# Issuing scores and value products one at a time between a unit's matmuls, in a one-core encoder block

## The chip, the cores and the metric

The kernel runs on one core of one Trainium2 chip. The time is the device time of one execution, in microseconds (us); the time of a kernel is the median of its runs. The engines are named as in the profile: PE is TensorE (matmuls; PEld its weight loads), DVE is VectorE, ACT is ScalarE, POOL is GpSimd, SP is SyncE, which here only issues transfers. Each engine works through its own instructions in the order in which the program wrote them and waits by semaphore for the others.

## The reference, cut to what matters

One encoder block on x of 256 tokens by 2048 channels, all in float32:

```python
h = rmsnorm(x, norm1_g)
q, k, v, u = split(h @ w_in)               # 12 q heads, 4 k and v heads of 128; u: 4 groups of 128
a = window_attention(q, k, v, sink)        # |t - s| <= 128, ALiBi, a sink logit per head
f = real(fft2(u, over positions and group channels)) @ w_fourier    # per group
x = x + concat(rmsnorm(a), rmsnorm(f)) @ w_out
h = rmsnorm(x, norm2_g)
gate, val = split(h @ w_up)                # 5504 each
x = x + (gelu(conv3(gate) + b) * val) @ w_down
y = rmsnorm(x, normf_g)
```

Attention is softmax over 256 keys for each of 12 heads: scores are q·k, masked and biased, the exponentials are divided by their sum plus that of the sink, and the result is multiplied by v.

## The kernel before

**Units.** The weights stream from memory in tiles of 128x2048 float32. Each tile is one *unit* of the first part: units 0 to 3 the u projection, 4 to 7 the v projection, 8 to 23 the k and q projections in the order k0 q0 q1 q2 k1 q3 … q11 (`QK_ORDER`), 24 to 39 the output projection. The feed-forward part follows and is not touched. A float32 product is made of three faster ones: every operand is split into a high part `hi` (a ScalarE copy to the faster format, L197) and the remainder `lo` (a VectorE subtraction, L205), and hi·hi, hi·lo and lo·hi are added. In a q/k unit (`still_weights`, L361) the weights stand in the array and the tokens stream: 16 matmuls of hi weights over 512 columns (both parts of the tokens) and 16 of lo weights over 256, alternately. In an output unit (`moving_weights`, L349) the tokens stand and 512 columns of weights stream, 24 matmuls.

**What sets the order.** The order on each engine is written out by hand in three tables of steps, `before`, `beside` and `behind`. `unit(i)` (L399) runs the steps of `before[i]`, issues the unit's matmuls, runs `beside[i]`, then `step(i)`, which issues the split of unit i+2 and the load of a later tile on SP, and then `behind[i]`. No scheduler moves anything: a step's place in these tables is its place in the order of every engine that it uses.

**The heads' steps.** A head whose q projection is unit s passes through these steps. At s+1, qk_out adds the two halves of its product and qk_parts splits it into qT (ScalarE, then VectorE). At s+2, `scores` (L743) makes six matmuls of 128x256 in `before`, `scores_out` masks them and takes the row maximum on VectorE, and `exps` makes exponentials on ScalarE, behind the split. At s+3, `weigh` divides them (VectorE L790) and `flip_out` transposes blocks of 32 (VectorE L336) and sends them to memory; at s+4 `flip_in` fetches them back turned. `flip_parts` splits the result into `pt` one unit ahead of `values`. `values` (L836) makes six matmuls of 128x256 with v in `before`, 7 units after the projection for heads 0 to 8, 6 for heads 9 and 10, 5 for head 11 (`values_at`), and `values_out` (feature_out: ScalarE square L550 and copy L298, VectorE L299, POOL add L554) puts the scaled parts into `cat`, the tokens of the output projection. Head 11 is not sent through memory: its exponentials are turned by TensorE (`turn`, L797) in `before` of unit 27, right after `weigh` of head 11 in unit 26.

**The Fourier group.** `fourier_rows` (position products, all in unit 9) are copied out by rows_out, two groups in unit 9 and two in unit 10. Then for g = 0 to 3 in unit 10+g: `fourier_channels` (channel products, on TensorE in `before`), `fourier_channels_copy` (ScalarE, beside), `fourier_channels_join` (VectorE L670 to L674, behind), and in unit 11+g `fourier_channels_out` (feature_out). `total_scale` (VectorE L561 to L579 and a POOL power L575) behind unit 25 makes the norm of the Fourier half.

**Buffers.** PSUM has two pools of four banks, `mm` for projections and `dn` for all the small products. The SBUF tags `tmp`, `add` and `sc` have 2, 2 and 4 buffers; the square of feature_out has one.

**Start.** A memset on POOL (L283) writes a 128x128 tile of ones, which TensorE multiplies 7 times (`WARM`) while the first loads are under way.

## Time and profile before

| | |
|---|---|
| median of 3 runs | 933.49 us (933.27 to 934.07) |
| the profiled execution | 933.83 us |
| its span, first to last instruction | 932.1 us |
| mean granted TensorE clock | 0.998 |
| busy PE / PEld / DVE / ACT / POOL | 923.2 / 799.9 / 776.2 / 543.6 / 62.8 us |
| PE's share of the chain that ended last | 98% |

How to read the rows: a row of the timeline has the start and the duration in us, engine, line, operation, output and inputs with their shapes and the count of equal instructions that it groups; at the end, in brackets, the idle time of the engine before it and what ended that. Matmuls overlap in the array, so a matmul's duration is longer than its share of the stream; what counts is the distance from start to start. Equal neighbours are one row (x6), whose duration is from the first start to the last end. Lines are those of the kernel before.

### The profile page before, as it was taken

The numbers are of one execution on the slowest core, as the hardware profiler recorded it, in microseconds if no ns is written. First come the engines' busy times: TensorE is split into PE (matmuls) and PEld (weight loads), VectorE is DVE, ScalarE is ACT, GpSimd is POOL, SyncE is SP. The second block draws the span as 40 slices with busy tenths as digits, with TensorE's granted clock in tenths as the row PEclk, the third lists the DMA queues.
The fourth block names the chain that finished last, engine by engine and source line by source line (L and its number), as shares of the span: only waits on it lengthen the run. The fifth ranks groups of instructions, "written<-read, shape, count | busy, mean of one in ns | idle before, by whom it ended". The sixth has DMA issues, their size and how long they took to land.

```text
span 932.1 us, 12883 instructions
## 1 busy us (share of the span) xinstructions
PE 923.2 (99%) x4973; PEld 799.9 (86%) x4973; DVE 776.2 (83%) x997; ACT 543.6 (58%) x689; POOL 62.8 (7%) x79
## 2 busy tenths in 40 slices
PE   9999999999999999999999999999999999999996
PEld 7888998888888888888888888888888888888885
DVE  7768998787768877898877997888978789989995
ACT  6756777546465655565555665555755556655553
POOL 0101111200000000000000000000000000000002
PEclk9999999999999999999999999999999999999999
DMA  9865777667777668788797769887787968779652
GB/s 361 331 225 158 249 241 215 201 198 269 230 274 256 203 207 256 242 274 263 229 299 251 240 209 298 223 260 233 268 240 244 306 221 269 237 238 272 203 180 91
DMA packets 59597, 225.16 MB, mean 242 GB/s; under 512 B 24465, under 2 KB 30225, under 8 KB 35984
## 3 DMA queue, kind: packets, MB, share of 16 engines
q1 hardware_dynamic: 54928, 194.72, 57.9%
q0 software_dynamic: 4464, 29.36, 17.0%
q8 instruction: 39, 0.64, 0.3%
q10 hardware_dynamic: 144, 0.26, 0.1%
q14 instruction: 22, 0.18, 0.0%
HBM read 216.98 MB, written 7.08 MB: 240 GB/s over the span
## 4 chain that ended last, share of the span: by engine, by line
PE 98%; DMA 0%; ACT 0%; DVE 0%; issue 0%; POOLq 0%; POOL 0%; ACTq 0%
PE ps_gate L372 25%; PE ps_val L372 25%; PE ps_q L372 7%; PE ps_P L1233 4%; PE ps_P L1234 4%; PE ps_P L1232 3%; PE ps_N L1233 3%; PE ps_N L1234 3%; PE ps_N L1232 3%; PE ps_k L372 2%; PE ps_a L357 2%; PE ps_a L355 2%; PE ps_a L356 2%; PE ps_s L748 1%; PE ps_o L842 1%; PE ps_ff L355 1%
## 5 line engine op out<-in xcount | busy, mean ns | idle before, releaser
L205 DVE TENSOR_TENSOR lo<-raw,hi 128x2048 fp32r<-128x2048 f32 (+2 forms) x133 | 295.0, 2221 | 28.3 <-ACT hi L197 28.0
L197 ACT ACTIVATE hi<-raw 128x2048 fp32r<-128x2048 f32 (+1 forms) x131 | 246.8, 1887 | 27.6 <-PE ps_a L356 10.8
L372 PE MATMUL ps_gate<-hU,hi 128*128 128x512 f32 x688 | 236.1, 389 | 0.0
L372 PE MATMUL ps_val<-hU,hi 128*128 128x512 f32 x688 | 236.1, 389 | 0.0
L372 PE MATMUL ps_gate<-hU,lo 128*128 128x256 f32 x688 | 189.9, 276 | 0.0
L372 PE MATMUL ps_val<-hU,lo 128*128 128x256 f32 x687 | 189.6, 276 | 0.0
L372 PEld LDWEIGHTS ps_gate<-hU,hi 128*128 128x128 f32 x688 | 129.2, 188 | 26.8
L372 PEld LDWEIGHTS ps_val<-hU,hi 128*128 128x128 f32 x688 | 129.2, 188 | 26.8
L372 PEld LDWEIGHTS ps_gate<-hU,lo 128*128 128x128 f32 x688 | 129.2, 188 | 1.3
L372 PEld LDWEIGHTS ps_val<-hU,lo 128*128 128x128 f32 x687 | 129.0, 188 | 1.3
L1013 ACT ACTIVATE ft_g<-ps_gate 128x256 f32<-128x256 f32 x43 | 16.5, 384 | 121.1 <-PE ps_gate L372 121.1
L1013 ACT ACTIVATE ft_v<-ps_val 128x256 f32<-128x256 f32 x43 | 16.5, 383 | 87.0 <-PE ps_val L372 87.0
L372 PE MATMUL ps_q<-hT,hi 128*128 128x512 f32 x192 | 65.0, 391 | 0.0
L1232 PE MATMUL ps_P<-hi_P,op_P 128*128 128x512 f32 x144 | 56.0, 389 | 0.0
L1233 PE MATMUL ps_P<-hi_P,op_P 128*128 128x512 f32 x144 | 56.0, 389 | 0.0
L1234 PE MATMUL ps_P<-lo_P,op_P 128*128 128x512 f32 x144 | 56.0, 389 | 0.0
L372 PE MATMUL ps_q<-hT,lo 128*128 128x256 f32 x192 | 51.2, 277 | 0.0
L1130 DVE TENSOR_TENSOR lo_N<-sumw,hi_N 128x2048 fp32r<-128x2048 f32 (+1 forms) x20 | 41.5, 2076 | 9.4 <-ACT hi_N L1129 9.2
L1232 PE MATMUL ps_N<-hi_N,op_N 128*128 128x512 f32 x108 | 42.0, 389 | 0.0
L1233 PE MATMUL ps_N<-hi_N,op_N 128*128 128x512 f32 x108 | 42.0, 389 | 0.0
L1234 PE MATMUL ps_N<-lo_N,op_N 128*128 128x512 f32 x108 | 42.0, 389 | 0.0
L372 PEld LDWEIGHTS ps_q<-hT,hi 128*128 128x128 f32 x192 | 35.2, 188 | 6.6
(415 smaller groups left out, 1592.4 us busy)
## 6 DMA issues: line engine op xcount, KB each, us to landing
raw<-in_w_up SPq DMA_DIRECT2D x86, 1024.0 KB, 6.6
raw<-in_w_in SPq DMA_DIRECT2D x20, 1024.0 KB, 5.4
raw<-in_w_out SPq DMA_DIRECT2D x16, 1024.0 KB, 5.1
sumw<-in_w_down POOLq DMA_DIRECT2D x16, 1024.0 KB, 8.6
raw<-in_w_down_late SPq DMA_DIRECT2D x4, 1024.0 KB, 6.8
raw<-in_w_down_last SPq DMA_DIRECT2D x4, 768.0 KB, 4.0
turnp<-flip SPq DMA_DIRECT2D x44, 64.0 KB, 1.9
flop<-turnp SPq DMA_DIRECT2D x11, 256.0 KB, 3.9
```

The costliest lines, as they stand in the source:

```text
L197: nc.scalar.activation(halves[i][0][:, s], raws[i][:, s], AF.Copy)
L205: nc.vector.tensor_tensor(lo[:, s], raws[i][:, s], f32(hi[:, s]), ALU.subtract)
L355: nc.tensor.matmul(ps, ah, wh, start=first and q == q0, stop=False)
L356: nc.tensor.matmul(ps, al, wh, start=False, stop=False)
L357: nc.tensor.matmul(ps, ah, wl, start=False, stop=last and q == q0 + len(kk) - 1)
L372: nc.tensor.matmul(ps[:, x], (hi, lo)[i][:, k * P : (k + 1) * P], hk(k)[:, x], start=n == 0 and k == 0, stop=n == len(order) - 1 and k == ...
L748: nc.tensor.matmul(ps[:, b * S : (b + 1) * S], qT[:, qo + b * P : qo + (b + 1) * P], kT[:, ko : ko + S], start=n == 0, stop=n == 2,)
L1013: nc.scalar.activation(tmp, ps[:, S : 2 * S], AF.Copy)
L1130: nc.vector.tensor_tensor(lo, src, f32(hi), ALU.subtract)
L1232: nc.tensor.matmul(ps, o[:, 0, p, :], hi[:, s], start=first and p == 0, stop=False)
L1233: nc.tensor.matmul(ps, o[:, 1, p, :], hi[:, s], start=False, stop=False)
L1234: nc.tensor.matmul(ps, o[:, 0, p, :], lo[:, s], start=False, stop=last and p == n - 1)
```

## The change

Scores and products with v are no longer issued as blocks ahead of a unit's matmuls. `scores` and `values` now return lists of six calls each; `unit` puts them on the list `woven`, scores first, and the unit's own loop takes one off it at a time: in a q/k unit after each lo matmul (16 places), in an output unit after each matmul (24 places). `turn` of head 11 stays in `before` of unit 27, now alone there. `values_out` moves behind the split in units below 24 and stays beside, ahead of `weigh`, from unit 24 on. The four channel products all stand ahead of unit 10; their copies and joins come two groups per unit in units 10 and 11, the outs two per unit in 11 and 12; all four rows_out are in unit 9. The warm-up multiplies a constant that the framework provides, 7 times in full and once with half the columns, and the memset of ones is gone. The calls and their shapes are otherwise the same.

```diff
-    ones = base.tile([P, P], F32, tag="ones", name="ones")
-    nc.gpsimd.memset(ones, 1.0)
...
-    ps = bank(dn, "ps_warm")
-    for _ in range(WARM):
-        nc.tensor.matmul(ps[:, 0:P], ones, ones, start=True, stop=True)
+    ps, one = bank(dn, "ps_warm"), nc.const_aps.tensor(1.0, (P, P), F32)
+    for n in [P] * WARM + [P // 2]:
+        nc.tensor.matmul(ps[:, 0:n], one, one[:, 0:n], start=True, stop=True)
...
+    woven = []
+
+    def weave():
+        if woven:
+            woven.pop(0)()
+
     def moving_weights(hi, lo, n, kk, act, b, ps, first, last, q0=0):
...
             nc.tensor.matmul(ps, ah, wh, start=first and q == q0, stop=False)
+            weave()
             nc.tensor.matmul(ps, al, wh, start=False, stop=False)
+            weave()
             nc.tensor.matmul(
                 ps, ah, wl, start=False, stop=last and q == q0 + len(kk) - 1
             )
+            weave()
...
+            if i:
+                weave()
...
     def unit(i, work):
         run(before, i)
+        for f, a in within.pop(i, []):
+            woven.extend(f(*a))
         work(*halves.pop(i))
+        assert not woven
         run(beside, i)
         step(i)
         run(behind, i)
...
         at(before, 9, fourier_rows, g)
-        at(beside, 9 + g // 2, fourier_rows_out, g)
+        at(beside, 9, fourier_rows_out, g)
...
-            i = 10 + g
-            at(before, i, fourier_channels, g)
-            at(beside, i, fourier_channels_copy, g)
-            at(behind, i, fourier_channels_join, g)
-            at(beside, i + 1, fourier_channels_out, g)
-        at(behind, N_OUT + 1, total_scale, sq_f, "f", FW)
+    i = N_QK + 2
+    for g in range(NG):
+        at(before, i, fourier_channels, g)
+        at(beside, i + 1 + g // 2, fourier_channels_out, g)
+    at(behind, N_OUT + 1, total_scale, sq_f, "f", FW)
...
+            at(beside, N_QK + 2 + g // 2, fourier_channels_copy, g)
+            at(behind, N_QK + 2 + g // 2, fourier_channels_join, g)
...
-        for n, h in sorted(heads.items()):
-            if n == values_at(h):
-                at(before, i, values, h)
         if 4 in heads and heads[4] not in FLIPS:
             at(before, i, turn, heads[4])
         if 2 in heads:
-            at(before, i, scores, heads[2])
+            at(within, i, scores, heads[2])
+        now = [h for n, h in sorted(heads.items()) if n == values_at(h)]
+        for h in now:
+            at(within, i, values, h)
...
-        for n, h in sorted(heads.items()):
-            if n == values_at(h):
+        if i >= N_OUT:
+            for h in now:
                 at(beside, i, values_out, h)
...
             at(behind, i, exps, heads[2])
+        if i < N_OUT:
+            for h in now:
+                at(behind, i, values_out, h)
```

More of the change, by code (lines that the diff above doesn't have):

```diff
@@ L1 @@
 from contextlib import ExitStack
+from functools import partial
 import concourse.bass as bass
@@ L386, in step @@
             split(i + ahead)
-    before, beside, behind = {}, {}, {}
+    before, beside, behind, within = {}, {}, {}, {}
     def at(when, i, f, *a):
@@ L694, in block_kernel @@
         at(before, 9, fourier_rows, g)
-        at(beside, 9 + g // 2, fourier_rows_out, g)
+        at(beside, 9, fourier_rows_out, g)
     at(behind, 8, distances)
-    def fourier_channels_steps():
-        for g in range(NG):
-            i = 10 + g
-            at(before, i, fourier_channels, g)
-            at(beside, i, fourier_channels_copy, g)
-            at(behind, i, fourier_channels_join, g)
-            at(beside, i + 1, fourier_channels_out, g)
-        at(behind, N_OUT + 1, total_scale, sq_f, "f", FW)
+    i = N_QK + 2
[3 more added lines that the diff above has]
+    at(behind, N_OUT + 1, total_scale, sq_f, "f", FW)
     ps_v = [bank(mm, f"ps_v{b}") for b in range(2)]
@@ L745, in scores, with one @@
         qT, kT = qk_sb.pop(("q", h)), qk_sb["k", h // GQA]
-        for b in range(2):
-            for n, (qo, ko) in enumerate([(0, 0), (0, S), (S, 0)]):
-                nc.tensor.matmul(
-                    ps[:, b * S : (b + 1) * S],
-                    qT[:, qo + b * P : qo + (b + 1) * P],
-                    kT[:, ko : ko + S],
-                    start=n == 0,
-                    stop=n == 2,
-                )
+        def one(b, n, qo, ko):
+            nc.tensor.matmul(
+                ps[:, b * S : (b + 1) * S],
+                qT[:, qo + b * P : qo + (b + 1) * P],
+                kT[:, ko : ko + S],
+                start=n == 0,
+                stop=n == 2,
+            )
+        parts = [(0, 0), (0, S), (S, 0)]
+        return [partial(one, b, n, *o) for b in range(2) for n, o in enumerate(parts)]
     def scores_out(h):
@@ L839, in values, with one @@
         ps = st["o", h] = bank(dn, f"ps_o{h}")
-        for sb in range(2):
-            for n, (v, q) in enumerate([(v_hi, 0), (v_hi, 1), (v_lo, 0)]):
-                nc.tensor.matmul(
-                    ps[:, 0:S],
-                    v[:, sb, g * HD : (g + 1) * HD],
-                    pt[q][:, sb * S : (sb + 1) * S],
-                    start=sb == 0 and n == 0,
-                    stop=sb == 1 and n == 2,
-                )
+        def one(sb, n, v, q):
+            nc.tensor.matmul(
+                ps[:, 0:S],
+                v[:, sb, g * HD : (g + 1) * HD],
+                pt[q][:, sb * S : (sb + 1) * S],
+                start=sb == 0 and n == 0,
+                stop=sb == 1 and n == 2,
+            )
+        parts = [(v_hi, 0), (v_hi, 1), (v_lo, 0)]
+        return [partial(one, sb, n, *o) for sb in range(2) for n, o in enumerate(parts)]
     def values_out(h):
@@ L855, in values_at, with fourier_channels_steps @@
         return 5 + 2 * (h in FLIPS) - (h in SOON)
+    def fourier_channels_steps():
+        for g in range(NG):
+            at(beside, N_QK + 2 + g // 2, fourier_channels_copy, g)
+            at(behind, N_QK + 2 + g // 2, fourier_channels_join, g)
     slot_of = {kh: N_QK + n for n, kh in enumerate(QK_ORDER)}
@@ L987, in block_kernel @@
     pa.close()
-    assert not (before or beside or behind), (before, beside, behind)
+    assert not (before or beside or behind or within), (before, beside, behind)
     fp = ctx.enter_context(tc.tile_pool(name="fp", bufs=2))
```

## The prediction

> **What bounds the kernel now.** I read the page's busy shares and its chain of work first, then one stretch of time around each edit, then the rows of the engines inside it.

> ```profile
> PE 923.2 (99%) x4973; PEld 799.9 (86%) x4973; DVE 776.2 (83%) x997; ACT 543.6 (58%) x689; POOL 62.8 (7%) x79
> PE 98%; DMA 0%; ACT 0%; DVE 0%; issue 0%; POOLq 0%; POOL 0%; ACTq 0%
> ```

> TensorE is busy for 923.2 of 932.1 us, and the chain that ended last is TensorE for 98%. So an edit pays only by shortening TensorE's own stream, and costs wherever TensorE comes to wait. The stretches are columns start:end, length, then busy time (instructions) of PE, PEld, DVE, ACT, POOL, the granted clock, DMA share, GB/s.

> ```profile
> 87.00:97.00 10.00, 10.00 (x62) 8.92 (x61) 9.34 (x22) 7.87 (x17) 2.43 (x3) 1.00 0.67 219
> 161.60:174.50 12.90, 12.90 (x67) 10.92 (x66) 10.43 (x29) 7.69 (x15) 3.79 (x4) 1.00 0.71 224
> ```

> TensorE never idles in the two stretches that the change touches most, at full clock, but VectorE has 9.34 of 10.00 us and 10.43 of 12.90 us of work there. Its reserve is what the argument turns on. All sums below are against the profiled execution, 933.83 us (932.1 of span and 1.73 around it), which is 0.34 above the median 933.49; I take the 0.34 off at the end. About 0.2%, 1.87 us, is what a measurement here can tell from no change.

> **The woven matmuls on TensorE.** Twelve score blocks and twelve value blocks of six 128x256 matmuls each now go one by one between others: 16 blocks in q/k units, 8 in units 24 to 28.

> ```profile
> 144.23 0.39 PE L372 MATMUL ps_q<-hT,hi 128*128 128x512 f32 x1
> 144.45 0.28 PE L372 MATMUL ps_q<-hT,lo 128*128 128x256 f32 x1
> 144.57 0.39 PE L372 MATMUL ps_q<-hT,hi 128*128 128x512 f32 x1
> ...
> 147.07 0.88 PE L748 MATMUL ps_s<-kT,qT 128*128 128x256 f32 x6
> 147.78 0.63 PE L372 MATMUL ps_q<-hT,hi 128*128 128x512 f32 x2
> ```

> Today a hi and a lo matmul take 0.34 us from start to start (144.23 to 144.57), and six score matmuls 0.71 us, 0.118 each. A woven q/k unit runs hi, lo, score: two 256-column matmuls in a row. The nearest rows are a unit opening where two lo stand in a row:

> ```profile
> 102.82 0.40 PE L372 MATMUL ps_k<-hT,lo 128*128 128x256 f32 x2
> 103.06 0.39 PE L372 MATMUL ps_k<-hT,hi 128*128 128x512 f32 x1
> ```

> Those two took 0.24, 0.12 each. The lo ahead costs 0.113 today (0.34 less 0.227 for the hi), so a woven matmul adds 0.113 if it is free of a seam and 0.127 if the pair always takes 0.24, against 0.118 in a chain: over 96 of them −0.5 to +0.9 us. I take +0.5, nearer to the pair's row, which is the same shape in a row of two, but stands where two units meet. In units 24 to 28 a 256 stands between two 512s, as a lo does today: 48 matmuls at 0.113 to 0.118 gain 0 to 0.2 us, and up to 0.4 with the ends of their eight blocks; I take −0.2. Together +0.3, from −0.9 to +0.9. The channel products are 16 matmuls of the same shapes in one place: 0.

> **Warm-up.** Reading a constant frees TensorE from the memset.

> ```profile
> 1.00 3.36 PE L291 MATMUL ps_warm<-ones 128*128 128x128 f32 x14 [1.00 <-POOL ones L283]
> 4.52 1.88 PE L429 MATMUL ps_u<-hi,hT 128*128 128x512 f32 x4 [0.16 <-ACT hT L298]
> 12.61 0.19 PEld L357 LDWEIGHTS ps_u<-lo,hT 128*128 128x128 f32 x1 [0.29 <-DVE lo L423]
> ```

> It can start some 0.26 us sooner and is lengthened by one half-size product, but the first real matmul waits 0.16 us for ScalarE's hT, whose input comes by DMA, and one at 12.61 waits 0.29 us for a lo tile: what is won ahead is lost there. 0, between −0.3 and +0.3.

> **The Fourier steps, units 9 to 15.** Joins (VectorE L670 to L674) and the outs (ScalarE L550, L298, POOL's add, VectorE L299) go from one group per unit in units 10 to 14 to two per unit in 10 to 12. TensorE loses nothing until a split or a q tile is late, and unit 15, whose scores now begin after its third matmul, is where it gets tight.

> ```profile
> 71.53 0.16 DVE L674 COPY y<-yh 128x2 f32<-128x2 f32 x1
> 71.61 0.42 DVE L727 TENSOR_TENSOR add_q<-ps_q,tmp_q 128x256 f32<-128x256 f32 x1
> 75.35 2.29 DVE L205 TENSOR_TENSOR lo<-raw,hi 128x2048 fp32r<-128x2048 f32 x1 [1.01 <-ACT hi L197]
> 82.47 2.29 DVE L205 TENSOR_TENSOR lo<-raw,hi 128x2048 fp32r<-128x2048 f32 x1
> 90.06 2.28 DVE L205 TENSOR_TENSOR lo<-raw,hi 128x2048 fp32r<-128x2048 f32 x1
> 92.26 0.28 DVE L670 TENSOR_TENSOR y<-yh 128x127 f32<-128x127 f32 x1
> 92.73 0.42 DVE L727 TENSOR_TENSOR add_q<-ps_q,tmp_q 128x256 f32<-128x256 f32 x1
> ...
> 93.18 0.42 ACT L298 ACTIVATE qT<-add_q 128x256 fp32r<-128x256 f32 x1 [1.67 <-DVE add_q L727]
> 93.51 0.40 ACT L550 ACTIVATE sq<-y 128x256 f32<-128x256 f32 x1
> 93.81 0.49 ACT L298 ACTIVATE cat<-y,vec 128x256 fp32r<-128x256 f32 x1
> 93.99 0.75 POOL L554 TENSOR_TENSOR sq_f<-sq_f,sq 128x256 f32<-128x256 f32 x1 [1.59 <-ACT sq L550]
> 94.73 0.88 PE L748 MATMUL ps_s<-kT,qT 128*128 128x256 f32 x6
> ```

> The three lo tiles are those of units 13, 14, 15. A join is 0.47 (92.26 to 92.73). In the changed order VectorE does two joins and then, at once, two cat instructions, each of which needs ScalarE's sq and cat of the same group (0.30 and 0.40 from start to start) and, for the second pass, POOL's 0.75 that frees the one sq buffer. Before, a group's cat came 2 us later, with ScalarE done. Pass one, ahead of unit 13's lo: one join more moves the end of the joins from 71.61 to 72.08, ScalarE needs to 73.1 for two groups, VectorE's cat to 73.55 where add_q stood at 71.61; behind it ScalarE's hi, hence lo, starts about 1.65 late (77.0). Pass two, ahead of unit 14's lo: again 0.87 of VectorE work and about 1.25 of waiting, 3.75 late (86.2), just in time for unit 14. Ahead of unit 15's lo one cat less: 2.95 late, 93.0. From there head 3's qT on ScalarE ends as today, 3.54 after lo's start (93.60 from 90.06), less the join that is gone, 0.47: 96.1. TensorE reaches its first woven score at 94.73 + 2×0.227 + 0.113 = 95.3. Cost 0.8. If ScalarE hides all hand-offs, VectorE's own extra there is one join and one cat, 0.87, and the slack covers it: 0. If every hand-off adds half as much again, 2.4.

> **Head 11's turn, units 25 to 27, the main term.** Head 11's exponentials are turned by TensorE (L797) at the start of unit 27; that needs VectorE's weigh of head 11, which stands behind values_out of heads 7 and 8, a split and total_scale.

> ```profile
> 160.77 0.28 PE L842 MATMUL ps_o<-pt,v_lo 128*128 128x256 f32 x1
> 161.15 0.39 ACT L550 ACTIVATE sq<-ps_o 128x256 f32<-128x256 f32 x1 [0.54 <-PE ps_o L842]
> 161.93 0.48 DVE L299 SCALAR_TENSOR_TENSOR cat<-ps_o,vec,cat 128x256 fp32r<-128x256 f32 x1 [0.62 <-ACT cat L298]
> ...
> 164.78 2.29 DVE L205 TENSOR_TENSOR lo<-raw,hi 128x2048 fp32r<-128x2048 f32 x1
> 166.99 0.44 DVE L561 STREAM_TRANSPOSE turned_f<-sq_f 128x256 f32<-128x256 f32 x1
> ...
> 168.68 0.73 ACT L832 ACTIVATE pt<-flop 128x256 fp32r<-128x256 f32 x2 [2.31 <-DMA flop<-turnp]
> ...
> 170.62 1.22 DVE L579 COPY rstdf<-sums_f 32x2 f32<-32x2 f32 x4 [1.77 <-POOL sums_f L575]
> ...
> 172.55 0.48 DVE L299 SCALAR_TENSOR_TENSOR cat<-ps_o,vec,cat 128x256 fp32r<-128x256 f32 x1
> 173.13 0.62 DVE L790 TENSOR_SCALAR sc<-sc,ex 128x256 f32<-128x256 f32 x2
> ...
> 169.20 0.40 PE L355 MATMUL ps_a<-hi,cat 128*128 128x512 f32 x1
> 173.07 0.40 PE L357 MATMUL ps_a<-lo,cat 128*128 128x512 f32 x1
> 174.01 0.60 PE L797 MATMUL ps_t<-ident,sc 128*128 128x128 f32 x4
> ```

> From head 7's last product (start 160.77) VectorE waits only twice, 0.62 for ScalarE and 1.77 for POOL; weigh ends at 173.75, and with the hand-off that TensorE's products show toward ScalarE (0.1 behind 161.05) the turn could start at 173.85, 13.08 after that product. It started at 174.01: the slack is 0.16. TensorE paces here at 0.228 a matmul (169.20 to 173.07 is 17 steps). In the changed kernel scores come first in unit 25's list and head 7's products after them, so the last stands behind the unit's twelfth matmul instead of ahead of its first; values_out(7) stays ahead of weigh, so all of VectorE's row behind it moves too. TensorE from there to the turn: 12 matmuls of unit 25 (2.73), 24 of unit 26 with six woven (5.46 and 0.68) and the product itself (0.11): 8.98. The turn also loses the 0.71 of head 9's block, which stood ahead of it and is now woven behind. Wait: 13.08 − 8.98 = 4.1 us. Nothing on TensorE can take its place: unit 27's matmuls stand behind the turn in its order. What could shorten it is a VectorE chain that closes up; the 1.77 on POOL and the 11 us of instructions have no gaps, so I allow 1.2 less, and 0.3 more for hand-offs: 2.9 to 4.4. The cover that remains: values_out(7) moves by 3.4 (12 matmuls and 6 woven in place of none), unit 27's lo then ends at about 170.5 and head 9's transfer, which released ScalarE at 168.68, comes at about 172.1, while VectorE gets to head 9's parts only behind total_scale, at about 175.2: neither is late. The other values_out steps, put behind the split below unit 24, feed nothing before the output projection: 0.

> **A rule that speaks against the wait.** TensorE's last matmul of the kernel started at 924.08 and took 0.28.

> ```profile
> 924.40:927.60 3.20, 0.00 (x0) 0.00 (x0) 2.19 (x6) 1.53 (x4) 0.75 (x2) 1.00 0.07 25
> 927.70:932.00 4.30, 0.00 (x0) 0.00 (x0) 0.00 (x0) 0.00 (x0) 0.00 (x0) 0.50 0.58 217
> ```

> The granted clock stood at 1.00 for 3.2 us of idling and at 0.50 from there. A wait of 4.1 us is longer than that idling. [...] If it halves, the next 3 us of matmuls run at half speed, 1.5 us lost (estimate: as long as the idling that the rows show, at 0.50). [...]

> **Sum.** 933.83 + 4.1 + 0.8 + 0.3 + 0 = 939.0, less 0.34: 938.7 us.

> **The rivals.**
> - The turn does not wait: weigh(11) is done when TensorE gets to unit 27, 0.7 before today's 174.01. That leaves 933.49 + 0.8 + 0.3 = 934.6, no slower by the bound above, and 933.4 with weaving at its lower bound. It takes 4.1 us out of the 13.08 of VectorE's row. For it speaks that VectorE has 2.5 us free in the second stretch above; against it, that 2.4 of these are the two waits within the row, which follow one on another. 0.06 for no slower, 0.02 for faster.
> - The change doesn't do what it says: the lists could be issued after a unit, as blocks again. The diff asserts that each unit has emptied its list and pops one at each matmul, so I give it nothing of its own.
> - Half of the turn's wait is absorbed, as its lower bound and some overlap between its instructions would: 2.0 + 0.8 + 0.3 over the median gives 936.6. 0.20.
> - The clock halves in the wait: 938.7 + 1.5 = 940.2. For it, the two windows above; against it, that the idle is only 0.8 longer than 3.3. 0.20.
> - Unit 15 waits its upper bound, 2.4: 938.7 + 1.6 = 940.3. For it, VectorE's 9.34 of 10.00; against it, that ScalarE has 2.1 us free there. 0.10.
> - The forecast itself, 937.5 to 939.6: 0.44.

> The range 935.9 to 940.9 holds the last four but for their tails: below it the turn costs under 1.3, above it two of the bounds meet. Slower by over 0.2% (above 935.36) is 0.92, within 0.06, faster 0.02.

> **What would show it.** TensorE idle of about 4 us before ps_t, released by VectorE's sc; of about 1 us near 95 before ps_s, released by ScalarE's qT; score and value matmuls starting 0.11 to 0.13 after the one ahead; lo tiles of units 13 to 15 some 2 to 4 us later. From unit 30 on everything is shifted and else unchanged. I am wrong if weigh(11) is ready when unit 27 begins, or if the wait is there but won back later.

## The result and the profile after

| | before | changed |
|---|---|---|
| median of 5 runs | 933.49 us (933.25 to 934.18) | 942.07 us (940.75 to 943.58) |
| the profiled execution | 933.83 us | 940.75 us |
| its span | 932.1 us | 939.0 us |
| mean granted TensorE clock (1 is full speed) | 0.998 in the profiled one | 0.998, 0.998, 0.995, 0.996, 0.996, from the shortest run to the longest |

The changed kernel is slower by a factor of 1.0088, 95% interval 1.0073 to 1.0103: 8.6 us where 5.2 were forecast, and above the range (935.9 to 940.9). Some runs of most kernels here, of the one before too, were lengthened by some 16 us by a disturbance; medians and ratios below leave them out, and of the profiles of e3, e7 and e8, which it fell on, only rows ahead of 250 us are read. The kernel before had medians of 933.7 to 934.1 in the later comparisons; each ratio is against its own, with the 95% interval in brackets behind it.

The page of the changed kernel, busy times and the chain of work that ended last:

```profile
PE 926.1 (99%) x4975; PEld 800.7 (85%) x4975; DVE 775.0 (83%) x997; ACT 544.0 (58%) x689; POOL 63.0 (7%) x78
PE 93%; DVE 4%; ACT 2%; issue 0%; DMA 0%; POOL 0%; POOLq 0%; DVEq 0%; ACTq 0%
```

VectorE and ScalarE, 0% of the chain before, now hold 6% of it, and TensorE is busy for 2.9 us more with the same matmuls but for one warm-up product. Its waits (tile, line, who ended it: us in total, times, longest):

```profile
PE ps_t L810 <- DVE sc L803: 3.5, 1, 3.5
PE ps_warm L290 <- PEq L1576: 0.8, 1, 0.8
PE ps_u L442 <- ACT hT L297: 0.4, 1, 0.4
PE ps_s L758 <- ACT qT L297: 0.3, 1, 0.3
```

The turn's wait is there. Both kernels issue the same matmuls within each unit, so the distance between the starts of a unit's last matmul in the two traces tells where the time came from. For the profiled execution, worked out from these starts:

| place | later than before by | grew here by |
|---|---|---|
| end of unit 4 | 0.38 | 0.38: the start |
| end of unit 15 | 1.63 | 1.25: waits in units 13 and 15, 1.0, woven matmuls 0.25 |
| end of unit 26 | 2.40 | 0.77: woven matmuls |
| end of unit 27 | 6.22 | 3.82: the turn, 3.7, and woven matmuls |
| end of unit 39 | 6.31 | 0.09: woven matmuls in unit 28 |
| second product of the feed-forward | 6.86 | 0.55: a lo tile is late there |

That is 6.9 us of the 8.6. Another 1.3 lie between this execution, the fastest of the five, and the median, and 0.3 between the profiled execution before and its median. For the 1.3 the last line of the first table says where to look: the longer runs have the lower clock.

The turn, in the changed kernel's timeline (TensorE, then VectorE):

```profile
166.56 0.28 PE L855 MATMUL ps_o<-pt,v_lo 128*128 128x256 f32 x1
...
175.47 0.39 PE L364 MATMUL ps_a<-lo,cat 128*128 128x512 f32 x1
179.38 0.72 PE L810 MATMUL ps_t<-ident,sc 128*128 128x128 f32 x4 [3.53 <-DVE sc L803]
```

```profile
167.71 0.49 DVE L298 SCALAR_TENSOR_TENSOR cat<-ps_o,vec,cat 128x256 fp32r<-128x256 f32 x1 [1.20 <-ACT cat L297]
...
170.56 2.29 DVE L206 TENSOR_TENSOR lo<-raw,hi 128x2048 fp32r<-128x2048 f32 x1
...
176.41 1.18 DVE L592 COPY rstdf<-sums_f 32x2 f32<-32x2 f32 x4 [1.77 <-POOL sums_f L588]
...
178.30 0.48 DVE L298 SCALAR_TENSOR_TENSOR cat<-ps_o,vec,cat 128x256 fp32r<-128x256 f32 x1
178.88 0.62 DVE L803 TENSOR_SCALAR sc<-sc,ex 128x256 f32<-128x256 f32 x2
```

Head 7's last product starts at 166.56, the turn 12.82 later; before, 13.08 was the sum. VectorE's row behind it is the one forecast, with the same wait for POOL. TensorE was busy for 9.14 of the 12.82 (to 175.70, the 0.227 of a 512 behind 175.47), not for 8.98, so 3.7 us are lost.

### The profile page after: what moved, and what is told of

It is laid out like the page before. It is cut to its first block, busy times and chain, and to the rows that moved or that the text cites. A ratio compares the mean times of both kernels' runs of the same rounds, so it can differ in the third digit from the quotient of the medians.

```text
span 939.0 us, 12895 instructions
## 1 busy us (share of the span) xinstructions
PE 926.1 (99%) x4975; PEld 800.7 (85%) x4975; DVE 775.0 (83%) x997; ACT 544.0 (58%) x689; POOL 63.0 (7%) x78
## 4 chain that ended last, share of the span: by engine, by line
PE 93%; DVE 4%; ACT 2%; issue 0%; DMA 0%; POOL 0%; POOLq 0%; DVEq 0%; ACTq 0%
PE ps_val L380 25%; PE ps_gate L380 25%; PE ps_q L380 4%; PE ps_P L1258 3%; PE ps_P L1256 3%; PE ps_P L1257 3%; PE ps_N L1258 3%; PE ps_N L1257 3%; PE ps_N L1256 3%; PE ps_a L364 2%; PE ps_a L362 2%; PE ps_a L360 2%; PE ps_k L380 2%; DVE lo L206 1%; PE ps_o L855 1%; PE ps_ff L364 1%
## 5 line engine op out<-in xcount | busy, mean ns | idle before, releaser
L380 PE MATMUL ps_q<-hT,hi 128*128 128x512 f32 x192 | 68.4, 392 | 0.0
```

What stands on the lines that cost most here:

```text
L380: nc.tensor.matmul(ps[:, x], (hi, lo)[i][:, k * P : (k + 1) * P], hk(k)[:, x], start=n == 0 and k == 0, stop=n == len(order) - 1 and k == ...
```

## The experiments

**e1: keep TensorE from idling in the wait.**

```diff
+        for _ in range(12):
+            nc.tensor.matmul(ps, v_hi[:, 0, 0:P], v_hi[:, 0, 0:512], start=True, stop=True)
         for sb in range(2):
             for b in range(2):
                 nc.tensor.transpose(
```

> The changed kernel with 12 idle products of 512 columns, about 2.7 us, put on TensorE ahead of the turn. In the changed kernel's profile TensorE idled 3.53 us there at full clock, and of its five runs the two shortest (940.75, 940.87) have a mean clock of 0.998, the three longer ones (942.07 to 943.58) 0.995 or 0.996. If the idling itself lowers the clock in some runs, the fill takes that away: all runs near 940.8, clock 0.998, median 1.2 us below the changed kernel's 942.07. If the longer runs have another cause, the median stays near 942 with the same scatter of about 3 us. The wait itself stays: if the fill shortened the time below 940.3, idling would cost in a way that neither theory has.

Measured: 939.90 us, all five runs between 939.83 and 939.98, clock 0.997 to 0.999; ratio 1.0064 (1.0052 to 1.0077). The turn starts when it did:

```profile
175.45 2.92 PE L809 MATMUL ps_t<-v_hi 128*128 128x512 f32 x12
179.15 0.72 PE L814 MATMUL ps_t<-ident,sc 128*128 128x128 f32 x4 [0.77 <-DVE sc L803]
```

So 12 useless products make the kernel 2.2 us shorter at the median, and the scatter of 2.8 us shrinks to 0.15. With the idling the lower clock is gone too, and the long runs with it; e9 will show that the idling is not the only source of scatter. The kernel ended 0.4 below my limit of 940.3, and 0.9 below the changed kernel's profiled execution; two things that this execution had are missing here: 0.36 at the start (unit 4 stands at +0.02, there at +0.38) and 0.55 in the feed-forward, where no lo tile is late.

**e4: the Fourier steps in their old places.** One group per unit in units 10 to 14, in the changed kernel.

> The changed kernel with the Fourier steps back in their old places (one group per unit, 10 to 14). By the profile the Fourier steps made units 13 and 15 late by 0.40 and 0.63 us: if so, this gives 942.07 - 1.0 = 941.0, or 939.7 where the clock does not fall in the wait of the turn. If those waits come from the weaving instead, nothing changes.

Measured: 941.31 us (940.30 to 941.95), 1.0079 (1.0065 to 1.0092), clock 0.993 to 0.995 in every run. Its profile caught the clock's fall. TensorE waits for nothing in units 10 to 15; up to the end of unit 26 it has lost 0.99 since unit 4, against 2.02 in the changed kernel: the Fourier steps cost 1.0 in that execution, as expected. In the records at hand the granted clock stands at one value for whole multiples of 3.413 us (one here, two in e8, 270 and 272 in the profiled executions of the kernel before and of the changed one, listed at the end), so I call a stretch of that length a window. The rows are the window ahead of the fall, the fall and what follows (columns as in the prediction):

```profile
175.40:178.80 3.40, 1.08 (x7) 1.01 (x8) 3.29 (x11) 1.17 (x3) 0.00 (x0) 1.00 0.25 91
178.80:182.20 3.40, 3.40 (x13) 2.83 (x12) 1.91 (x3) 0.22 (x1) 0.00 (x0) 0.50 0.36 72
182.20:186.00 3.80, 3.80 (x18) 3.15 (x17) 2.12 (x3) 2.83 (x4) 0.74 (x1) 1.00 0.51 216
```

The wait is 3.56 us in this profile, and the turn starts at 177.72. From 178.82 on, 1.1 us behind it, TensorE runs at half clock for 3.41 us: 13 matmuls in 3.40 us where the next 3.80 hold 18. Unit 27 ends 5.39 later against unit 26 than before, 1.57 more than the 3.82 without the fall.

**e8: weaving from unit 24 on alone**, in the kernel before: there is no crowding ahead of it and the warm-up is the old one.

```diff
+        if i < N_OUT:
+            for h in now:
+                at(before, i, issue, values, h)      # all six at once, as before
...
+        if i < N_OUT:
+            if 2 in heads:
+                at(before, i, issue, scores, heads[2])
+        else:
             if 2 in heads:
                 at(within, i, scores, heads[2])
             for h in now:
                 at(within, i, values, h)
```

> The kernel before with weaving from unit 24 on alone. The wait of the turn stands here, 3.5 or a little less, with 0.09 in each of five units and the late start of the feed-forward, 0.5: 938.0; where the clock falls behind the wait, 939.3 and a wider scatter. If the prediction's step is right in its size, 4.1 - 0.2 = 937.4. If the wait needs VectorE to be late from the units before, 936 or less.

Measured: 940.30 us (939.15 to 943.15), 1.0067 (1.0047 to 1.0086), clock 0.994 to 0.996 in all. This edit alone brings three quarters of the loss, 1.0 us more than I had expected with a fall of the clock. The wait is as long as in the changed kernel, so it needs no lateness from earlier units, and here the fall lasts for two windows (6.83 us, 175.70 to 182.53):

```profile
172.30:175.70 3.40, 1.04 (x5) 0.54 (x3) 1.74 (x6) 2.72 (x4) 2.25 (x2) 1.00 0.90 345
175.70:182.50 6.80, 5.61 (x19) 4.85 (x20) 4.14 (x8) 1.31 (x4) 0.12 (x1) 0.50 0.33 110
182.50:186.00 3.50, 3.50 (x17) 2.87 (x16) 2.18 (x3) 2.46 (x3) 0.62 (x1) 1.00 0.22 94
```

```profile
176.89 1.09 PE L815 MATMUL ps_t<-ident,sc 128*128 128x128 f32 x4 [3.55 <-DVE sc L808]
...
178.42 0.63 PE L364 MATMUL ps_a<-hi,cat 128*128 128x512 f32 x1
178.84 0.41 PE L860 MATMUL ps_o<-pt,v_hi 128*128 128x256 f32 x1
179.06 0.63 PE L366 MATMUL ps_a<-lo,cat 128*128 128x512 f32 x1
```

A 512 and a 256 take 0.64 us (178.42 to 179.06) instead of 0.35. Unit 27 grows by 6.34, 2.5 more than without the fall.

**e9: a shorter idle time.** As e1 with 4 products.

> The changed kernel with 4 instead of 12 idle products ahead of the turn: TensorE then idles 2.8 us there in place of 3.7 (from the last product's end in its stream to the turn) or 0.9. The clock changes in steps of 3.413 us in the records so far; of these windows, those with 1.88 us of idling kept full speed and those with 2.31 and 2.52 lost it. If a window loses its speed from some 2 us of idling on, then 2.8 us of idling still cost the clock in about half of the runs: clock 0.995 or 0.996 and 1.5 to 2.5 us more in these, 939.9 in the others. If a whole window must be idle, as I took it in the prediction, no run can lose it: all at 939.9 and 0.997 to 0.999, as with 12 products.

Measured: 940.66 us (939.95 to 941.92), 1.0071 (1.0058 to 1.0084), clock 0.997 to 0.999, as in the kernel before, which has no such wait: no run of the five shows a fall. The profile has two stretches of 3.40 us that share the idle time (that the edge of a window lies at 178.30 is my count of steps of 3.413 us; the rows, at full clock on both sides, don't show it),

```profile
174.90:178.30 3.40, 1.74 (x8) 1.09 (x6) 1.98 (x7) 2.45 (x4) 2.16 (x3) 1.00 0.84 327
178.30:181.70 3.40, 2.47 (x15) 2.21 (x16) 3.36 (x6) 0.72 (x2) 0.00 (x0) 1.00 0.02 5
```

and kept its clock with 1.66 of 3.40 us idle in the fuller one. This execution is the longest of the five, 941.92, for other reasons:

```profile
PE ps_s L758 <- ACT qT L297: 1.0, 2, 0.8
PE ps_val L380 <- DVE lo L206: 0.9, 1, 0.9
```

From unit 4 to the end of unit 15 this execution loses 1.9 us where the changed kernel's lost 1.25, because the scores wait longer for qT, and at the feed-forward's opening, where a lo tile is late, 1.9 where that lost 0.6. So the clock need not be the only source of the changed kernel's scatter.

**e2: products with v ahead of the scores from unit 24 on.**

> The changed kernel with the list of unit 24 on turned round: products with v first, scores behind. Head 7's last product then stands behind the sixth matmul of unit 25, six pairs of 0.35 us sooner. If VectorE's row from that product to the turn is what TensorE waits for, the wait falls from 3.53 to about 1.5 us, too short to lower the clock: 938.7, from 938.2 to 939.2, clock 0.998. If the wait is set by something else (head 9's transfer, the exponentials of head 11), it stays and the time with it, 940.8 to 942.

Measured: 938.33 us, from two runs only, 937.42 and 939.24, one on either side of the range expected; 1.0048 (1.0030 to 1.0065), clock 0.998 in both.

```profile
PE ps_t L810 <- DVE sc L803: 1.4, 1, 1.4
```

The wait fell by 2.1 us for a product that comes 2.1 us sooner (six pairs of 0.353): VectorE's row from that product is what TensorE waits for. In the profiles of e4, e8 and e12, too, the turn comes 12.85 to 12.87 us behind that product.

**e3: total_scale of the Fourier half out of that row.** `at(behind, N_OUT + 3, total_scale, …)` instead of `N_OUT + 1`.

> The changed kernel with total_scale of the Fourier half put behind unit 27 instead of 25, out of VectorE's row ahead of the turn; its 4.8 us there (1.77 of them a wait for POOL) exceed the wait of 3.53. If the row is what TensorE waits for, the wait is gone, and the clock's loss and what VectorE carries late into the feed-forward (0.55) with it: 940.75 - 3.5 - 0.5 = 936.7, from 936.3 to 937.3. If only the part up to head 9's pieces counts, some 1 us of wait stays: 937.7 or more.

Measured: 939.83 us (939.24 to 941.36), 1.0066 (1.0053 to 1.0079). I missed the first case by 3 us; the wait came out as in the second. One of the four runs, 941.36, has a mean clock of 0.995, which the wait in the profile, 1.07, doesn't explain. The wait fell, but only to 1.07; the next to end last is head 9's transfer (ScalarE, then VectorE):

```profile
174.18 0.73 ACT L845 ACTIVATE pt<-flop 128x256 fp32r<-128x256 f32 x2 [2.28 <-DMA flop<-turnp]
174.63 0.76 DVE L846 TENSOR_TENSOR pt<-flop,pt 128x256 fp32r<-128x256 f32 x2 [2.03 <-ACT pt L845]
```

In the profile TensorE is 3.6 us later than before at the end of unit 39, but the runs ended 5.4 us or more later. VectorE is 6.5 us late in units 30 to 33 with total_scale put there, which would make the feed-forward's opening late. That the rest is lost there is argued from this lateness, not shown.

**e5: only the Fourier steps moved**, in the kernel before.

> The kernel before with only the Fourier steps moved. TensorE's matmuls are the same, the four products cost 0.45 each in either place. If the crowding of VectorE and ScalarE alone makes unit 15 late: 934.5, from 934.1 to 935.0. In the kernel before the scores stand ahead of unit 15's matmuls, 0.57 earlier than when woven, so the wait for head 3's qT could be longer than in the changed kernel. If the waits need the weaving too: 933.5.

Measured: 935.80 us (935.64 to 936.13), 1.0016 (1.0006 to 1.0025): 1.5 us by the ratio, where 1.0 was expected. The crowding alone costs more than it does with weaving, and it does so two units sooner than I had looked:

```profile
83.96 1.20 PE L745 MATMUL ps_s<-kT,qT 128*128 128x256 f32 x6 [1.28 <-ACT qT L298]
```

These are head 2's scores, ahead of unit 13. In the changed kernel the same scores stand behind three matmuls of the unit, and their wait is 0.45, seen on the weight load (first row; the second is head 3's wait in unit 15):

```profile
84.46 0.19 PEld L758 LDWEIGHTS ps_s<-kT,qT 128*128 128x128 f32 x1 [0.45 <-ACT qT L297]
...
96.73 0.39 PE L758 MATMUL ps_s<-kT,qT 128*128 128x256 f32 x1 [0.31 <-ACT qT L297]
```

**e6: only the warm-up.**

> The kernel before with only the warm-up reading the constant. In the changed kernel's profile unit 4 began 0.38 us later than before. If that is the longer warm-up: 933.9. If it was only how the first transfers and the clock fell in that run: 933.5, from 933.2 to 933.8, as predicted.

Measured: 933.78 us (933.23 to 934.89), 0.9996 (0.9986 to 1.0005): nothing. The 0.38 at the start of the changed kernel's profile belongs to that execution; the profiles of the other kernels stand between −0.61 and +0.16 there.

**e7: weaving in units 8 to 23 alone.**

> The kernel before with weaving in units 8 to 23 alone (values_out behind the split there), blocks from unit 24 on, in the old order. By the changed kernel's profile a unit loses 0.04 with six woven matmuls and 0.10 with twelve: ten of score blocks and six with value blocks as well make about +0.9: 934.4, from 934.1 to 934.9. As predicted for these units: +0.5, 934.0.

Measured: 934.80 us (934.17 to 936.21), 1.0006 (0.9997 to 1.0016): as expected, but by the time alone not to be told from no change. In its profile these units cost 0.76, 0.04 to 0.07 with six woven matmuls and 0.08 to 0.10 with twelve, as in the changed kernel.

**e10: does the change of PSUM bank make a woven matmul dear?**

```diff
+            if ps_lo is not None:
+                nc.tensor.matmul(
+                    (ps, ps_lo)[i][:, x], (hi, lo)[i][:, k * P : (k + 1) * P], hk(k)[:, x],
+                    start=k == 0, stop=k == NK - 1,
+                )
+                continue
```

> The kernel before with the lo matmuls of units 8 to 23 accumulating in a second PSUM bank (which nobody reads: the part of q and k that the low parts of their weights give is left out). TensorE then changes the bank at each of 512 matmuls, with the same operands and shapes. A hi and a lo take 0.340 us in one bank; a 512 and a woven 256 in two banks took 0.355 in the changed kernel. If the change of bank is what makes woven matmuls dear: 256 pairs by 0.010 to 0.015, 936.1 to 937.4. If the cost comes from the operands of scores and values (other tiles, other weights): 933.5, from 933.2 to 934.2.

Measured: 933.78 us, 0.9996 (0.9986 to 1.0005). In these q/k units the bank changes at every matmul and the pair stays at 0.34:

```profile
104.65 0.39 PE L373 MATMUL ps_k<-hT,hi 128*128 128x512 f32 x1
104.87 0.28 PE L373 MATMUL ps_lok<-hT,lo 128*128 128x256 f32 x1
104.99 0.39 PE L373 MATMUL ps_k<-hT,hi 128*128 128x512 f32 x1
```

**e11: does it come from the operands?** 24 extra products of 256 columns in each of units 30 to 37.

> The kernel before with 24 extra products of 256 columns in each of units 30 to 37, one behind each matmul, into a bank that nobody reads. Units 30 and 31 take both operands from the unit itself; 32 and 33 both from v; 34 and 35 the standing one from v, the streaming one from the unit; 36 and 37 the reverse. A 512 and a 256 stream for 0.340 us; with woven scores the pair took 0.353 to 0.357. If the mere alternation in an output unit costs the 0.015, all four forms take 0.355. If foreign operands cost it, units 30 and 31 stay at 0.340 and one of the mixed forms names the operand. The time of the whole is 8 x 24 x 0.113 = 21.8 us more with no meaning of its own.

Measured (one run, 958.2 us): the pairs took 0.353, 0.353, 0.351 and 0.353 us in the four forms, means over 47 pairs each from the starts. With a unit's own operands:

```profile
195.93 0.40 PE L369 MATMUL ps_ff<-hi,cat 128*128 128x512 f32 x1
196.17 0.28 PE L360 MATMUL ps_extra<-lo,cat 128*128 128x256 f32 x1
196.28 0.40 PE L371 MATMUL ps_ff<-lo,cat 128*128 128x512 f32 x1
196.53 0.28 PE L360 MATMUL ps_extra<-hi,cat 128*128 128x256 f32 x1
196.65 0.40 PE L367 MATMUL ps_ff<-hi,cat 128*128 128x512 f32 x1
```

In an output unit a 512 and a 256 take 0.011 to 0.013 more than the 0.340 that they take in a q/k unit, whatever the 256 reads. It always wrote to another bank than the 512s here; e10 speaks against the bank, but in q/k units, and a 256 into the same bank was not tried in an output unit. Why the same alternation costs less in a q/k unit stays open.

**e12: the changed kernel with two steps undone**, the Fourier steps of e4 and the order of e2.

> The changed kernel with two of its steps undone: the Fourier steps in their old places, and products with v ahead of the scores from unit 24 on. What stays is weaving (0.76 in units 8 to 23, 0.45 from 24 on) and a wait of the turn of 1.5, too short for the clock: 933.9 + 2.7 = 936.6, from 936.0 to 937.6, clock 0.997 to 0.999. If the parts don't add up (a wait that one of them had hidden comes out): 938 or more, or below 935.5.

Measured: 937.08 us (936.43 to 937.22), 1.0035 (1.0022 to 1.0048), clock 0.998 in all. The parts add up. What is left, weaving, a wait of 1.5 us and, in the profile, 0.7 at the feed-forward's opening, is still 3.4 us behind the kernel before. None of the kernels beat that one.

## Why the prediction was wrong, point by point

- **What bounds the kernel, and the direction:** right. Only TensorE's stream and its waits count.
- **Head 11's turn, 4.1 us:** right in place, mechanism and nearly in size: 3.7 measured. e8 has it alone, e2 moves it by just what the row says, and e3 shortens it until the next wait ends it. VectorE's row was 12.82 rather than 13.08, and TensorE was slower to get there by 0.16. The cover that I named, head 9's transfer, holds only 2.5 us: it comes next (e3).
- **The rule that speaks against the wait:** this step failed. I read the two rows at the kernel's end as "3.3 us of idling are needed", about a whole window, gave the fall 0.2 and left it out of the sum. The rows show only that the clock had fallen 3.3 us after the last matmul, not that less would not do. At the end of e10 it fell after 2.3 us of idling (the last matmul ends at 923.90), and after as much at the end of e4 (930.82 to 933.17):

```profile
923.90:926.20 2.30, 0.00 (x1) 0.00 (x0) 1.45 (x5) 0.78 (x3) 0.74 (x2) 1.00 0.00 0
926.30:928.00 1.70, 0.00 (x0) 0.00 (x0) 0.65 (x1) 0.71 (x2) 0.00 (x0) 0.50 0.59 213
```

  By the mean clocks the fall came in 3 of the 5 runs, in all 5 of e4 and all 4 of e8, and in none of e1, e2, e9 or e12 with 0.8 to 2.8 us of idling; the one run of e3 with 0.995 stays unexplained. The median lies 1.3 above the profiled execution, which kept its clock. That this is the clock's is argued from the three lower clocks and from e1; no profile of the changed kernel caught a fall. My price for a fall, 1.5, was near: 1.6 and 2.5 measured. What was wrong is its chance: 3.3 us of idling were not needed. Two windows with 2.32 and 2.36 of 3.40 us idle (3.40 less the busy 1.08 and 1.04 above) lost the clock, while the changed kernel's profiled execution, whose wait the edge at 177.58 cut in two (50 steps of 3.413 us behind 6.92, where its record of full clock begins), kept it:

```profile
174.20:177.60 3.40, 1.66 (x8) 1.04 (x6) 1.51 (x7) 3.16 (x5) 2.50 (x3) 1.00 0.92 317
177.60:181.00 3.40, 1.62 (x11) 1.45 (x11) 3.34 (x7) 0.73 (x2) 0.00 (x0) 1.00 0.17 59
```

  with 1.74 and 1.78 us idle, 3.5 together. An estimate from these rows, with the edge equally likely at every place: if a window loses the clock from x us of idling on, an idle time of 3.5 us escapes only when neither of its two parts exceeds x, for 2x − 3.5 out of 3.41 us of places for the edge. At x = 2.1, between the 1.78 that kept the clock and the 2.32 that lost it, that is 0.7 of 3.41, about one run in five. Of the 14 runs with that wait two escaped.
- **The woven matmuls, +0.3:** mis-sized. 1.2 measured: 0.76 in units 8 to 23, within the bounds of −0.5 to +0.9 but near the upper one that the row of two lo gave, and +0.4 from unit 24 on where I took −0.2. The sum lies above my upper bound for the whole term, +0.9. The failing assumption is that a 256 between two 512s costs no more there than a lo does in a q/k unit; e11 measured 0.353 against 0.340.
- **The Fourier steps, 0.8:** the size was right (1.0 against e4, in one execution each), the place half. The size moves from execution to execution: less some 0.25 for weaving, the profiles of e2 and e9, which keep the moved steps, lose 0.6 and 1.6 up to the end of unit 15. I followed the lo tiles and head 3's qT to unit 15 and overlooked head 2's qT for unit 13, which waits first. My lateness of the three lo tiles (1.65, 3.75, 2.95) was short by some 0.2 to 0.6: in the trace they start 2.2, 4.4 and 3.2 later than before, less the 0.38 of the start.
- **Warm-up, 0:** right (e6).
- **"From unit 30 on everything is shifted and else unchanged":** wrong by 0.55 in the profiled execution. VectorE stays 1.7 us behind TensorE's new place after the turn, the blocks that go through memory come back later, and the feed-forward's second product waits for a lo tile (ScalarE, changed kernel, then before):

```profile
250.20 1.71 ACT L971 ACTIVATE hU<-flipx2lo,vec 128x256 fp32r<-128x256 f32 x4 [6.17 <-DMA flipx2lo<-turnx]
```

```profile
242.09 1.71 ACT L947 ACTIVATE hU<-flipx2lo,vec 128x256 fp32r<-128x256 f32 x4 [4.37 <-DMA flipx2lo<-turnx]
```

  8.1 us later where TensorE is 6.3 later. It doesn't happen in every execution: in those of e1 and e2 nothing is lost there, in that of e9 1.9.

Together: 3.7 + 1.2 + 1.0 + 0.55 + 0.38 = 6.8 for the profiled execution and 1.3 more at the median, in the main for the clock, as argued above. Without that 1.3 the time would have been 940.8, just within the range. By this account the clock took the time out of it, and the woven matmuls (0.9 too low) and the two places set at nothing (0.55 and 0.38) brought it to the edge; a turn that came 0.4 cheaper hid a part. Among the chances, those of the four cases that are clearly slower add up to 0.94, where the last line of the forecast says 0.92; nothing hangs on it. The single changes (e5, e6, e7, e8) give +1.5, −0.4, +0.6 and +6.3 by their ratios, 8.0 against 8.2 for the whole.

## What to carry to other kernels

A step that is spread out ends later than the block that it was, and whoever reads its last instruction gets it that much later: head 7's last product started at 166.56 instead of 160.77, with TensorE as a whole only 1.6 to 2.4 us late there (ends of units 15 and 26). Follow the last instruction, not the first, through the rows of the engines behind it. A wait on TensorE of some 3.5 us had a second price here, because the clock fell behind it in 12 of 14 runs; it showed as a scatter of the changed kernel's runs with their mean clock (940.75 at 0.998 to 943.58 at 0.996), and the profile of the fastest run, at 0.998, hid it. Price an interleaving by the same pair of shapes in the same kind of unit: the row of another kind was off by 0.013 us a pair, which was two thirds of the error in this term.
